# Router's logits from rows without the norm; scale and shift of the mixture's norm applied to gathered rows and to the residual

## The chip, the core and the metric

The kernel runs on one core of one Trainium2 chip. The time is that of one execution on the device in microseconds (us). The core has TensorE (PE, matrix products), VectorE (DVE), ScalarE (ACT), GpSimd (POOL) and SyncE (SP, whose queue starts the weight transfers), each with its own instruction stream, and 16 DMA engines. An instruction starts when those before it on its engine have gone and the semaphores that it waits for have come.

## The reference

Two layers work on 256 rows of width 2048. Each layer has a mixer and a mixture of experts, and after each of them the norm of the residual sum:

```
for i in range(2):
    mix = s5_mixer(h) if i == 0 else dsa_mixer(h)
    h = layer_norm(ALPHA * h + mix, ln_mix_g[i], ln_mix_b[i])
    ffn = hier_moe(h, ...)
    h = layer_norm(ALPHA * h + ffn, ln_ffn_g[i], ln_ffn_b[i])

def layer_norm(x, g, b): return (x - mean) * rsqrt(var + eps) * g + b

def hier_moe(x):
    group  = top 1 of softmax(x @ w_group + b_group)            # 4 groups
    expert = top 2 of softmax(x @ w_expert + b_expert) in group  # 8 each
    y = sum over the two experts: gate * (silu(x @ w_gate) * (x @ w_up)) @ w_down
```

All of it is in float32. There are 32 experts; each has three matrices of 2 MB.

## The kernel before

The rows stand in `acc`, 128 partitions by two halves `h` of 128 rows by 2048 columns. A plan list holds every weight tile of the program in the order of use, 2 MB each (4096 floats in each of 128 partitions). `issue()` starts the DMA of the next tile of the plan on SP's queue, into one of six ring slots (or a spare one in the mixture); SP waits there until the slot is released by the last reader of its old tile. `take()` hands the oldest tile to the code. In each layer the list holds, ahead of the mixture's 96 weight tiles, a tile `gb` with gain and bias of the mixer's norm, broadcast to all partitions (L143, L144).

The end of the mixer accumulates the output projection into `acc` and takes its statistics. Then the mixture begins (`moe`):

- *Norm.* `centre(q, h)` (L862) computes (acc - mean) * g on quarter q of the columns, `shift(q, h)` (L866) multiplies by `rs` = 1/sigma, from three Newton steps, and adds b: each eight times on 128x512 elements, on VectorE.
- *Logits.* While the quarters are being centred, TensorE transposes them (L222) into `xT` (ScalarE copies them from PSUM) and multiplies by the router weights `wr` of 36 columns (L1041) into `pl`. The factor `rs` and the bias are applied to the logits afterwards; `bw` (L1003, on GpSimd) is b times the router weights, whose column sums, by two products, go into `rbias`.
- *Split of the rows.* After each shift ScalarE rounds the rows to `xr` (L1058), and VectorE makes the rest `xl` (L1062). `keep_warm(p, n)` is n products without use.
- *Routing.* VectorE makes the logits `gl` and `el` (L1085, L1087), the group maximum `gr` (L1088), the choice (L1091 to L1104), positions within experts, and one-hot rows `ohr` (L1161).
- *Quads.* Eight quads of four experts: `gather` selects up to 32 rows for each expert by products of `xr`, `xl` with `ohr` and copies them to `xs` (L1178); `gate_up` (L1272) makes gate and up products, four experts side by side in columns of 32; `st_down` the down products; `scatter` adds them to `acc` (L1243). In quad 0 the scatter multiplies the old rows by ALPHA. `gate_up` runs over two halves of the contraction, in each over k = 0 (gate), 1 (up), and calls `issue()` twice after each k.

The order on each engine is that of the code, with lists of closures (`fill`, `during`) that put single steps between others.

Of the kernel before, what the change touches and what calls it, by code (L numbers as in the profile page):

```python
# [18 lines left out]
D = 2048  # L19
# [35 lines left out]
def kernel(ctx: ExitStack, tc: tile.TileContext, A, out):  # L55
# [85 lines left out]
    def gb(g, b, i):  # L141
        def f(t):
            nc.sync.dma_start(t[:, 0:D], dram(A[g], i * D, [[0, P], [1, D]]))  # L143
            nc.sync.dma_start(t[:, D:2 * D], dram(A[b], i * D, [[0, P], [1, D]]))  # L144
        return f

    def plan_s5():
# [12 lines left out]
        plan.append(gb("ln_mix_g", "ln_mix_b", 0))  # L160
# [682 lines left out]
    def ln_start(stt):  # L843
        if isinstance(stt, tuple):
            stt, gbt = stt
        else:
            gbt = take()
# [5 lines left out]
        return mv, ve, gbt[:, 0:D], gbt[:, D:2 * D]  # L853
# [91 lines left out]
    def plan_moe(li):  # L945
# [17 lines left out]
        i = RING - 1  # L963
# [6 lines left out]
    def moe(li, stt):  # L970

        with ExitStack() as ph:
# [14 lines left out]
            xT = [prp.tile([P, 4, L], F32, name="xT0")]  # L987
            wge = prp.tile([P, KC, 4], F32, name="wge")
            wex = prp.tile([P, KC, NEXP], F32, name="wex")
            wr = prp.tile([P, KC, 36], F32, name="wr")  # L990
            G.dma_start(wge, dram(A["moe_w_group"], li * D * 4, [[KC * 4, P], [4, KC], [1, 4]]))
            G.dma_start(wex, dram(A["moe_w_expert"], li * D * NEXP, [[KC * NEXP, P], [NEXP, KC], [1, NEXP]]))
            bT = prp.tile([P, KC], F32, name="bT")
            G.dma_start(bT, dram(A["ln_mix_b"], li * D, [[KC, P], [1, KC]]))
            rbias = prp.tile([P, 36], F32, name="rbias")
            G.dma_start(rbias[:, 0:32], dram(A["moe_b_expert"], li * 32, [[0, P], [1, 32]]))
            G.dma_start(rbias[:, 32:36], dram(A["moe_b_group"], li * 4, [[0, P], [1, 4]]))
# [4 lines left out]
            bw = prp.tile([P, KC, 36], F32, name="bw")  # L1002
            G.tensor_tensor(bw, wr, bT[:, :, None].to_broadcast([P, KC, 36]), op=OP.mult)  # L1003
# [17 lines left out]
            gl = sm("gl", [P, 2, 16]); el = sm("el", [P, 2, 40])  # L1021
            rp = sm("rp", [P, 2, 2, 8]); gr8 = sm("gr8", [P, 2, 8])
            for t in (gl, el, rp, gr8):
                G.memset(t, PAD)
            G.tensor_copy(id8, ident[0:8, 0:8])
# [3 lines left out]
            sbw = prp.tile([P, 36], F32, name="sbw")  # L1029
            xT += [prp.tile([P, 4, L], F32, name=f"xT{i}") for i in range(1, 4)]  # L1030
# [4 lines left out]
            junk, pbw = (pjk.tile([P, 512], F32, name="junk") for _ in range(2))  # L1035
            cut = lambda t, q: t.rearrange("p (k c) -> p k c", c=KC)[:, :, 4 * q:4 * q + 4]

            def logits(c0):
                for c in range(c0, c0 + 2):
                    for h in range(2):  # L1040
                        T.matmul(pl[:, h, 0:36], xT[c // 4][:, c % 4, h * 128:(h + 1) * 128], wr[:, c, :], start=c + h == 0,  # L1041
                                 stop=c == KC - 1, skip_group_check=True)


            for k in range(2):
                mm(pbw[:, 0:288], ones.to_broadcast([P, P]), bw[:, 8 * k:8 * k + 8].rearrange("p c n -> p (c n)"), k == 0, k == 1)
            keep_warm(pmm.tile([P, 512], F32, name="mm"), 8)
            centre, shift, rs = layer_norm(stt)
# [5 lines left out]
            def st_h(q):  # L1054
                for h in range(2):
                    shift(q, h)
                for h in range(2):
# [813 lines left out]
```

## Time and profile before

| | us |
|---|---|
| median of three runs | 1743.78 |
| lowest and highest | 1741.39, 1744.92 |
| the profiled execution's own time | 1746.2 |
| its span | 1744.6 |

Over the span TensorE is busy for 1500.0 us (86%), VectorE for 766.7 (44%), ScalarE for 498.3 (29%), GpSimd for 100.8 (6%); the mean granted clock of TensorE is 0.913. The DMA engines read 509.97 MB from HBM. TensorE's busy time includes products that run beside each other and ends that are modelled, so it is no measure of what is left to gain.

How to read the rows below: a timeline has the start in us from the span's start, the length, the engine, the line in the code, the operation, output<-inputs, elements, the count of instructions in the row, and in brackets the idle time ahead of it and who ended it. "x128" in one row are 128 records; a float32 product has two records. In the windows five pairs of busy time and count follow the length (PE, PEld, DVE, ACT, POOL); PEclk is the granted clock as a share of 2.4 GHz, behind it stand the DMA share and GB/s. Rows by form have busy us and the mean ns of one behind the first bar.

### The profile page before, as it was taken

To read this page: it belongs to the slowest core of one execution; us is meant where nothing else is said; L and a number is where in the kernel's file an instruction comes from. 1 tells how busy PE (TensorE), PEld (TensorE's weight loads), DVE (VectorE), ACT (ScalarE), POOL (GpSimd) and SP (SyncE) were. 2 spreads that over 40 slices of the span, in tenths; PEclk is the share of its full clock that TensorE was granted. 3 is DMA by queue.
4 is the path that set the end of the run, shared out by engine and by line. 5 is a ranking of instruction groups with operands and counts; after the bars stand their busy time and mean duration, and the time that the engine had idled before them with its cause. 6 is when DMAs were issued, how large, how long until landed. Compare 5 with 4: busy or idle time off the path is not lost. (4 is left out here: it accounts for less than half of the span.)

```text
span 1744.6 us, 28856 instructions
## 1 busy us (share of the span) xinstructions
PE 1500.0 (86%) x12151; PEld 1054.5 (60%) x12151; DVE 766.7 (44%) x1644; ACT 498.3 (29%) x1048; POOL 100.8 (6%) x225
## 2 busy tenths in 40 slices
PE   8899999999987777677788999999986887887687
PEld 7788888988643433343346998988743443433343
DVE  5788888666521112012116677976820220122015
ACT  2455554543310000000012464644410000010011
POOL 2111100001000000000001000500200000000000
PEclk8999999999887888898898999999988878888898
DMA  9545235655599999999996735344499999999994
GB/s 291 180 99 130 78 122 185 209 194 227 229 415 387 421 421 416 424 404 406 409 416 245 291 100 191 111 158 179 181 412 424 385 420 424 418 407 422 425 410 192
DMA packets 112939, 517.20 MB, mean 296 GB/s; under 512 B 8368, under 2 KB 41376, under 8 KB 71072
## 3 DMA queue, kind: packets, MB, share of 16 engines
q1 hardware_dynamic: 109664, 507.93, 73.5%
q0 software_dynamic: 3136, 7.31, 2.3%
q8 instruction: 100, 1.64, 0.4%
q14 instruction: 39, 0.32, 0.1%
HBM read 509.97 MB, written 5.24 MB: 295 GB/s over the span
## 5 line engine op out<-in xcount | busy, mean ns | idle before, releaser
L1272 PE MATMUL gu<-ring,xs 128*32 128x256 f32 x4096 | 319.5, 435 | 105.0 <-DMA ring<-in_moe_w_up_dram 84.9
L1272 PEld LDWEIGHTS gu<-ring,xs 128*32 128x32 f32 x4096 | 149.1, 124 | 263.3 <-DMA ring<-in_moe_w_up_dram 111.5
L64 PE MATMUL yd<-ring,hT 128*32 128x512 f32 x1024 | 190.8, 759 | 60.4 <-DMA ring<-in_moe_w_down_dram 59.4
L1197 DVE SCALAR_TENSOR_TENSOR hh<-gu,gsl,sg 128x256 f32<-128x256 f32 x16 | 7.7, 484 | 434.6 <-ACT sg L1195 434.6
L80 DVE TENSOR_TENSOR spl<-ring,spr 128x512 fp32r<-128x512 f32 x184 | 127.7, 696 | 83.7 <-ACT spr L79 80.3
L64 PE MATMUL mm<-ohr,xr 128*128 128x128 f32 x512 | 129.2, 294 | 32.5 <-DVE ohr L1161 19.1
L79 ACT ACTIVATE spr<-ring 128x512 fp32r<-128x512 f32 x184 | 115.7, 631 | 116.9 <-DVE spl L80 52.0
L64 PEld LDWEIGHTS yd<-ring,hT 128*32 128x32 f32 x1024 | 37.8, 131 | 180.1 <-DMA ring<-in_moe_w_down_dram 89.4
L80 DVE TENSOR_TENSOR yl<-yd,yr 128x512 fp32r<-128x512 f32 x64 | 44.3, 692 | 215.9 <-ACT yr L79 215.9
L64 PEld LDWEIGHTS mm<-ohr,xr 128*128 128x128 f32 x512 | 106.8, 209 | 45.1 <-issue 41.4
L64 PE MATMUL mm<-ohr,xl 128*128 128x128 f32 x512 | 128.5, 293 | 0.0
L1178 ACT ACTIVATE xs<-mm 128x512 f32<-128x512 f32 x64 | 38.2, 597 | 313.3 <-PE mm L64 313.3
L64 PE MATMUL u<-xT,ring 128*128 128x256 f32 x512 | 123.6, 396 | 2.1 <-DMA ring<-in_s_w_in_dram 1.6
L79 ACT ACTIVATE yr<-yd 128x512 fp32r<-128x512 f32 x64 | 38.3, 599 | 268.5 <-PE yd L64 268.5
L64 PEld LDWEIGHTS u<-xT,ring 128*128 128x128 f32 x512 | 98.7, 198 | 17.5 <-DMA ring<-in_s_w_in_dram 2.0
L64 PEld LDWEIGHTS mm<-ohr,xl 128*128 128x128 f32 x512 | 107.3, 209 | 0.1
L1195 ACT ACTIVATE sg<-gu 128x256 f32<-128x256 f32 x16 | 6.1, 384 | 254.1 <-PE gu L1272 254.1
L1243 DVE TENSOR_TENSOR acc<-acc,ps 128x512 f32<-128x512 f32 x112 | 72.7, 681 | 10.1 <-PE ps L64 10.0
L64 PE MATMUL ps<-yr,sc 128*128 128x512 f32 x128 | 59.2, 462 | 3.0 <-DVE acc L1243 2.0
L64 PEld LDWEIGHTS ps<-yr,sc 128*128 128x128 f32 x128 | 24.2, 189 | 61.2 <-issue 56.9
L1263 DVE TENSOR_SCALAR sc<-mm,slotp 128x256 fp32r<-128x256 f32 x16 | 7.7, 484 | 103.7 <-PE mm L64 103.7
L64 PE MATMUL mm<-spr,q 128*128 128x512 f32 x128 | 51.2, 400 | 0.0
(408 smaller groups left out, 2618.0 us busy)
## 6 DMA issues: line engine op xcount, KB each, us to landing
ring<-in_moe_w_gate_dram SPq DMA_DIRECT2D x128, 1024.0 KB, 16.0
ring<-in_moe_w_up_dram SPq DMA_DIRECT2D x128, 1024.0 KB, 19.6
ring<-in_moe_w_down_dram SPq DMA_DIRECT2D x56, 2048.0 KB, 24.6
ring<-in_s_w_glu_dram SPq DMA_DIRECT2D x8, 2048.0 KB, 9.4
ring<-in_s_w_out_dram SPq DMA_DIRECT2D x8, 2048.0 KB, 8.3
ring<-in_moe_w_down_dram SPq DMA_DIRECT2D x16, 1024.0 KB, 19.9
ring<-in_dsa_w_out_dram SPq DMA_DIRECT2D x8, 2048.0 KB, 8.0
ring<-in_s_w_in_dram SPq DMA_DIRECT2D x7, 2048.0 KB, 10.6
```

The lines of the kernel that those rows point to most:

```text
L64: T.matmul(o, l, r, start=start, stop=stop)
L79: S.activation(dst[0], src, AF.Copy)
L80: V.tensor_tensor(dst[1], src, dst[0].bitcast(F32), op=OP.subtract)
L1178: S.activation(xs[:, 4 * q:4 * q + 4], p.rearrange("p (a b) -> p a b", a=4), AF.Copy)
L1195: S.activation(sg, gu[:, 0:FF], AF.Silu)
L1197: V.scalar_tensor_tensor(hh, gu[:, FF:2 * FF], g, sg, op0=OP.mult, op1=OP.mult)
L1243: V.tensor_tensor(acc[:, h, bs], acc[:, h, bs], ps, op=OP.add)
L1263: V.tensor_scalar(scs[qd], p[:, 0:L], slotp, None, op0=OP.is_equal)
L1272: T.matmul(gu[es, k * FF:(k + 1) * FF], xss[qd][:, 8 * half + c, es], w[e // 2][:, e % 2, c, :], start=half + c + k == 0, stop=half == 1 a ...
```

## The change

The logits are taken from the rows as they are: with wr = g * w, x the raw row, m its mean, the logit is rs * (x @ wr - m * sum(wr)) + sum(b * w) + bias. The rows themselves get only (x - m) * rs; gain and bias come later.

- *Router weights.* GpSimd makes `wr` = w * g and `wb` = w * b, laid out in 44 columns padded to 64, and adds up 16 parts of each to one (`sw`); a product with ones gives the column sums in all partitions. ScalarE's two copies into `wr` go.
- *Logits.* Transposes of `acc` start after the statistics; four products of a block go alternately to partitions 0 and 64 of `plT`, with the weights as the fixed operand (64 columns) and 256 rows moving. `plS` is its copy, and two products with `sel` (the identity on both halves) bring it back to rows, `pl`. 12 `keep_warm` products follow where there were 16, and the 8 ahead of the transposes go.
- *Norm.* Four operations of 128x1024 on VectorE (`st_z`) replace 16 of 128x512.
- *Gathered rows.* Each copy of 128x512 becomes four of 128x128 with gain and bias per partition (`gTc`); in the first two gathers two of the four are on VectorE.
- *Residual.* In quad 0, during k = 0 of the second half, `residual(c - 8)` runs after each of the eight steps: four products spread ALPHA * g or ALPHA * b over the partitions, two VectorE operations apply it to `acc`. GpSimd prepares the two vectors (`mix_parts`). The scatter of quad 0 becomes the plain sum.
- *Tiles.* The `gb` tile leaves the plan, and so does the `issue()` behind the shifts; the spare tile is the seventh of the mixture instead of the sixth.

```diff
@@ plans
-        plan.append(gb("ln_mix_g", "ln_mix_b", 0))
...
-        i = RING - 1
+        i = RING
@@ moe
-            S.activation(wr[:, :, 0:32], wex, AF.Copy)
-            S.activation(wr[:, :, 32:36], wge, AF.Copy)
+            gTc = sm("gTc", [P, 2, KC])
+            for i, n in enumerate(("ln_mix_g", "ln_mix_b")):
+                G.dma_start(gTc[:, i], dram(A[n], li * D, [[KC, P], [1, KC]]))
+            wr = prp.tile([P, KC, 64], F32, name="wr")
+            wb = prp.tile([P, KC, 44], F32, name="wb")
+            G.memset(wr, 0.0)
+            G.memset(wb, 0.0)
+            for i, t in ((0, wr), (1, wb)):
+                for w, a, n in ((wex, 0, 32), (wge, 40, 4)):
+                    G.tensor_tensor(t[:, :, a:a + n], w, gbT[:, i, :, None].to_broadcast([P, KC, n]), op=OP.mult)
...
-            G.tensor_tensor(bw, wr, bT[:, :, None].to_broadcast([P, KC, 36]), op=OP.mult)
+            G.tensor_tensor(sel, ident[:, 0:56], ident[:, 64:120], op=OP.add)
+            sw = prp.tile([P, 8, 2, 44], F32, name="sw")
+            for i, t in ((0, wr), (1, wb)):
+                G.tensor_tensor(sw[:, :, i], t[:, 0:8, 0:44], t[:, 8:16, 0:44], op=OP.add)
+            for n in (4, 2, 1):
+                G.tensor_tensor(sw[:, 0:n], sw[:, 0:n], sw[:, n:2 * n], op=OP.add)
...
+            gs56 = prp.tile([P, 56], F32, name="gs56")
+            G.memset(gs56, 0.0)
...
+            def logits(b):
+                for c in range(4 * b, 4 * b + 4):
+                    o = 64 * (c % 2)
+                    T.matmul(plT[o:o + 64, 0:L], wr[:, c, :], xT[b][:, c % 4, :], start=c < 2, stop=c >= KC - 2,
+                             skip_group_check=True)
...
+            def sums():
+                V.tensor_copy(gs56[:, 0:44], junk[:, 0:44])
+                V.tensor_tensor(rbias[:, 0:44], rbias[:, 0:44], junk[:, 44:88], op=OP.add)
...
-            keep_warm(junk, 16)
-            for q in range(4):
-                st_h(q)
-            issue()
+            keep_warm(plT, 12)
...
+            def st_z(h):
+                for k in range(2):
+                    s = slice(k * 1024, (k + 1) * 1024)
+                    V.tensor_scalar(acc[:, h, s], acc[:, h, s], mv[:, h, 0:1], rs[:, h:h + 1], op0=OP.subtract, op1=OP.mult)
...
+            st_z(0)
+            st_z(1)
+            sums()
...
+                V.scalar_tensor_tensor(lg[:, h], gs56, nm[:, h:h + 1], pl[:, h, 0:56], op0=OP.mult, op1=OP.add)
...
+                V.scalar_tensor_tensor(lg[:, h], lg[:, h], rs[:, h:h + 1], rbias, op0=OP.mult, op1=OP.add)
@@ gather
-                S.activation(xs[:, 4 * q:4 * q + 4], p.rearrange("p (a b) -> p a b", a=4), AF.Copy)
+                for c in range(4):
+                    k = 4 * q + c
+                    g, b = gTc[:, 0, k:k + 1], gTc[:, 1, k:k + 1]
+                    if first and c % 2:
+                        V.tensor_scalar(xs[:, k], p[:, c * P:(c + 1) * P], g, b, op0=OP.mult, op1=OP.add)
+                    else:
+                        S.activation(xs[:, k], p[:, c * P:(c + 1) * P], AF.Identity, scale=g, bias=b)
@@ quad 0
+            def residual(k):
+                b, i = divmod(k, 2)
+                p = pmm.tile([P, 512], F32, name="mm")
+                for j in range(2):
+                    for x in range(2):
+                        mm(p[:, j * 256:(j + 1) * 256], id8[:, 2 * b + j:2 * b + j + 1].to_broadcast([8, P]),
+                           mixp[x][:, i * 256:(i + 1) * 256], x == 0, x == 1)
+                for h in range(2):
+                    a = acc[:, h, b * CB:(b + 1) * CB]
+                    V.tensor_tensor(a, a, p, op=OP.add if i else OP.mult)
...
-                    gate_up(0, 1)
+                    gate_up(0, 1, lambda c: residual(c - 8))
```

The instructions of GpSimd at the beginning of layer 0's mixture, before. `gb_4484` holds gain and bias of the later norm (L1007), `slot_4507` a counting row.

```order
L996 DMA rbias<-in_moe_b_expert_dram 128x32
L997 DMA rbias<-in_moe_b_group_dram 128x4
L1001 MEMSET ones 128x1
L1003 TENSOR_TENSOR bw<-wr,bT 128x576
L1007 DMA gb_4484<-in_ln_ffn_g_dram 8x256
L1007 DMA gb_4484<-in_ln_ffn_b_dram 8x256
L1009 IOTA slot_4507 128x64
```

After the change the same place has these rows, from the DMA of `gTc` on:

```order
L995 DMA gTc<-in_ln_mix_g_dram 128x16
L995 DMA gTc<-in_ln_mix_b_dram 128x16
L1000 MEMSET wr 128x1024
L1001 MEMSET wb 128x704
L1004 TENSOR_TENSOR wr<-wex,gbT 128x16x32
L1004 TENSOR_TENSOR wr<-wge,gbT 128x16x4
L1004 TENSOR_TENSOR wb<-wex,gbT 128x16x32
L1004 TENSOR_TENSOR wb<-wge,gbT 128x16x4
L1006 MEMSET ones 128x1
L1008 TENSOR_TENSOR sel<-ident 128x56
L1011 TENSOR_TENSOR sw<-wr 128x8x44
```

The single product `bw` has become two DMAs and nine more instructions up to `sw`. Three further sums into `sw`, the two DMAs of the later norm, the small constants and then `MEMSET gs_4541 128x56` follow; before, nothing of the logits stood behind `bw`.

TensorE, from the last product of layer 0's output projection on, before:

```order
L64 MATMUL mm<-spl,sTr 128x512
L64 MATMUL junk<-bw,ones 128x288 x2
L64 MATMUL mm<-ident 128x128 x8
L222 MATMUL mm<-ident,acc 128x128 x8
L1041 MATMUL pl<-wr,xT_4485 128x36 x4
L222 MATMUL mm<-ident,acc 128x128 x4
L1041 MATMUL pl<-wr,xT_4485 128x36 x4
L222 MATMUL mm<-ident,acc 128x128 x4
L1041 MATMUL pl<-wr,xT_4533 128x36 x4
L222 MATMUL mm<-ident,acc 128x128 x4
```

And after; `junk<-xT, wr` are the logits' products into `plT`, a tile on one PSUM buffer of that name:

```order
L64 MATMUL mm<-spl,sTr 128x512
L1064 MATMUL mm<-ident,acc 128x128 x16
L1053 MATMUL junk<-xT_4546,wr 64x256 x4
L1064 MATMUL mm<-ident,acc 128x128 x8
L1053 MATMUL junk<-xT_4547,wr 64x256 x4
L1064 MATMUL mm<-ident,acc 128x128 x8
L1053 MATMUL junk<-xT_4548,wr 64x256 x4
L64 MATMUL junk<-sw,ones 128x88
L1053 MATMUL junk<-xT_4549,wr 64x256 x4
L64 MATMUL pl<-sel,plS 128x56 x2
L64 MATMUL junk<-ident 128x128 x12
```

The 16 first transposes follow the projection at once, ahead of any logits; sixteen logits products stand where there were 32, then the two small products with `sel`.

VectorE, from the last Newton step to the group maximum, before:

```order
L840 SCALAR_TENSOR_TENSOR rs_y<-rs_t,rs_y 128x2
L862 SCALAR_TENSOR_TENSOR acc<-acc,ln_mv,ring 128x128x4 x4
L1073 TENSOR_REDUCE sbw<-junk 128x36
L1074 TENSOR_TENSOR rbias<-rbias,sbw 128x36
L866 SCALAR_TENSOR_TENSOR acc<-acc,rs_y,ring 128x128x4 x8
L1085 SCALAR_TENSOR_TENSOR gl<-pl,rs_y,rbias 128x4 x2
L1087 SCALAR_TENSOR_TENSOR el<-pl,rs_y,rbias 128x32 x2
L1088 TENSOR_REDUCE gr_4524<-gl 128x2
```

And after:

```order
L833 SCALAR_TENSOR_TENSOR rs_y<-rs_t,rs_y 128x2
L1090 TENSOR_SCALAR acc<-acc,ln_mv,rs_y 128x1024 x4
L1073 COPY gs_4541<-junk 128x44
L1074 TENSOR_TENSOR rbias<-rbias,junk 128x44
L1106 SCALAR_TENSOR_TENSOR lg<-gs_4541,nm,pl 128x56 x2
L1108 SCALAR_TENSOR_TENSOR lg<-lg,rs_y,rbias 128x56 x2
L1109 TENSOR_REDUCE gr_4538<-lg 128x2
```

The centre and shift rows are gone, among them the four between the Newton steps; four operations on 1024 columns, which wait for the transposes, stand ahead of the sums and the logits.

## Rows read from the trace of the kernel before

**Rows 1.** Windows of layer 0: stretch, length, busy by engine, PEclk, DMA share, GB/s

```profile
438.00:446.00 8.00, 8.00 (x72) 8.00 (x72) 7.93 (x20) 5.19 (x7) 0.00 (x0) 1.00 0.01 4
...
452.00:463.00 11.00, 11.00 (x122) 7.13 (x124) 7.99 (x26) 4.73 (x10) 0.00 (x0) 0.69 0.09 14
463.00:501.00 38.00, 32.31 (x318) 17.99 (x310) 7.46 (x20) 4.85 (x9) 0.00 (x0) 0.87 1.00 422
...
505.00:900.00 395.00, 300.96 (x2720) 155.74 (x2724) 59.13 (x122) 36.35 (x66) 0.00 (x0) 0.86 0.99 412
```

**Rows 2.** Timeline of SP in layer 0

```profile
445.19 17.05 SPq L926 DMA_DIRECT2D ring<-in_moe_w_up_dram  x4
...
461.43 0.80 SPq L926 DMA_DIRECT2D ring<-in_moe_w_up_dram  x2
462.33 3.36 SPq L942 DMA_DIRECT2D ring<-in_moe_w_down_dram  x3
...
475.17 0.33 SPq L942 DMA_DIRECT2D ring<-in_moe_w_down_dram  x1
```

**Rows 3.** Timeline of VectorE (DVE), router of layer 0

```profile
436.53 2.73 DVE L862 SCALAR_TENSOR_TENSOR acc<-acc,ln_mv,ring 128x512 f32<-128x512 f32 x4
...
439.78 5.38 DVE L866 SCALAR_TENSOR_TENSOR acc<-acc,rs_y,ring 128x512 f32<-128x512 f32 x8
...
445.66 0.15 DVE L1088 TENSOR_REDUCE gr<-gl 128x2 f32<-128x8 f32 x1
```

**Rows 4.** Timeline of TensorE (PE), router and first gather of layer 0

```profile
428.44 0.39 PE L64 MATMUL mm<-spl,sTr 128*128 128x512 f32 x1
...
450.59 0.30 PE L64 MATMUL mm<-ohr,xr 128*128 128x128 f32 x1 [1.73 <-DVE ohr L1161]
...
452.63 0.27 PE L64 MATMUL mm<-ohr,xr 128*128 128x128 f32 x1
...
469.79 8.80 PE L1272 MATMUL gu<-ring,xs 128*32 128x256 f32 x128
```

**Rows 5.** Timeline of GpSimd (POOL), layer 0

```profile
428.91 0.19 POOL L1009 IOTA slot<- 128x64 f32 x1 [0.79 <-PE mm L64]
...
430.93 0.18 POOL L1025 CAST id<-ident 8x8 fp32r<-8x8 f32 x1
```

**Rows 6.** Groups of instructions by form, whole span: busy us, mean ns

```profile
L1272 PE MATMUL gu<-ring,xs 128*32 128x256 f32 x4096 | 319.5, 435 | 105.0 <-DMA ring<-in_moe_w_up_dram 84.9 <-DMA ring<-in_moe_w_gate_dram 20.1
...
L64 PE MATMUL u<-xT,ring 128*128 128x256 f32 x512 | 123.6, 396 | 2.1 <-DMA ring<-in_s_w_in_dram 1.6 <-ACT uT L388 0.5
...
L1730 POOL TENSOR_TENSOR hk<-hk,idx 128x256 f32<-128x256 f32 x16 | 12.3, 772 | 1.3
...
L1003 POOL TENSOR_TENSOR bw<-wr,bT 128x576 f32<-128x576 f32 x2 | 2.3, 1157 | 79.4 <-ACT wr L999 79.4
...
L481 POOL MEMSET eb<- 128x512 f32 x3 | 1.4, 514 | 0.0
...
L1646 DVE TENSOR_SCALAR cc<-cc,rs_y 128x512 f32<-128x512 f32 x2 | 0.9, 480 | 0.0
...
L347 ACT ACTIVATE kk<-iot,cmag,pp 128x128 f32<-128x128 f32 x64 | 30.9, 483 | 0.2 <-DVE p L577 0.2
```

**Rows 7.** Timelines of GpSimd, TensorE, VectorE and SP, router of layer 1

```profile
1226.00 0.54 POOL L991 DMA_DIRECT2D wge<-in_moe_w_group_dram  x1 [88.93 <-PE mm L64]
...
1239.12 1.59 POOL L1027 TENSOR_TENSOR gbl<-gb,gbr 8x512 fp32r<-8x512 f32 x1
...
1231.12 0.40 PE L64 MATMUL mm<-spl,q 128*128 128x512 f32 x1
...
1237.83 4.10 DVE L862 SCALAR_TENSOR_TENSOR acc<-acc,ln_mv,ring 128x512 f32<-128x512 f32 x4
...
1248.32 0.15 DVE L1088 TENSOR_REDUCE gr<-gl 128x2 f32<-128x8 f32 x1
...
1263.91 0.80 SPq L926 DMA_DIRECT2D ring<-in_moe_w_up_dram  x2
```

More of the change, by code (lines that the diff above doesn't have):

```diff
@@ L843, in ln_start, with ln_moments @@
     def ln_start(stt):
[L844 to L847, printed above, removed]
+        stt, gbt = stt
+        mv, ve = ln_moments(stt)
+        return mv, ve, gbt[:, 0:D], gbt[:, D:2 * D]
+    def ln_moments(stt):
         mv = lnp.tile([P, 2, 2], F32, name="ln_mv")
@@ L1027, in moe @@
             G.tensor_tensor(gbl, gb8, gbr.bitcast(F32), op=OP.subtract)
-            sbw = prp.tile([P, 36], F32, name="sbw")
-            xT += [prp.tile([P, 4, L], F32, name=f"xT{i}") for i in range(1, 4)]
+            xT = [prp.tile([P, 4, L], F32, name=f"xT{i}", tag="xT", bufs=2) for i in range(4)]
             xr = one.tile([P, 2, D], F32R, name="xr")
@@ L1034, in moe @@
             pjk = pool(pre, "mjk", 2, side="right", **PS)
[L1035 to L1042, printed above, removed]
@@ L1045, in moe @@
[L1045 to L1048, printed above, removed]
+            junk, plT = (pjk.tile([P, 512], F32, name="junk") for _ in range(2))
+            def logits(b):
[3 more added lines that the diff above has]
+                             skip_group_check=True)
@@ new lines, in moe @@
+            mv, ve = ln_moments(stt)
+            for b in range(NBLK):
+                for c in range(0, 4, 2):
+                    p = pmm.tile([P, 512], F32, name="mm")
+                    for c2 in range(2):
+                        for h in range(2):
+                            T.transpose(p[:, c2 * 256 + h * 128:c2 * 256 + (h + 1) * 128],
+                                        acc[:, h, b * CB + c + c2:(b + 1) * CB:4], ident)
+                    S.activation(xT[b][:, c:c + 2, :], p.rearrange("p (a b) -> p a b", a=2), AF.Copy)
+                if b:
+                    logits(b - 1)
@@ new lines, in moe @@
+            mm(junk[:, 0:88], ones.to_broadcast([P, P]), sw[:, 0].rearrange("p i n -> p (i n)"), True, True)
+            nm = sm("nm", [P, 2])
+            def sums():
+                V.tensor_copy(gs56[:, 0:44], junk[:, 0:44])
+                V.tensor_tensor(rbias[:, 0:44], rbias[:, 0:44], junk[:, 44:88], op=OP.add)
+            rs = newton_rsqrt(ve, 2, [lambda: V.tensor_scalar(nm, mv[:, :, 0], -1.0, None, op0=OP.mult)])
+            logits(NBLK - 1)
+            plS = prp.tile([P, L], F32, name="plS")
@@ L1051, in moe @@
+            S.activation(plS, plT[:, 0:L], AF.Copy)
+            for h in range(2):
+                mm(pl[:, h, 0:56], plS[:, h * 128:(h + 1) * 128], sel, True, True)
+            keep_warm(plT, 12)
             xcut = lambda t, h, q: t[:, h].rearrange("p (c k) -> p c k", c=KC)[:, 4 * q:4 * q + 4]
             ccut = lambda t, h, q: t[:, h].rearrange("p (k c) -> p c k", c=KC)[:, 4 * q:4 * q + 4]
[L1054 to L1057, printed above, removed]
-                    S.activation(xcut(xr, h, q), ccut(acc, h, q), AF.Copy)
+            def st_z(h):
+                for k in range(2):
+                    s = slice(k * 1024, (k + 1) * 1024)
+                    V.tensor_scalar(acc[:, h, s], acc[:, h, s], mv[:, h, 0:1], rs[:, h:h + 1], op0=OP.subtract, op1=OP.mult)
@@ L1166, in xs_tile, with gather @@
                 return wk.tile([P, KC, P], F32, name="xs")
-            def gather(ohr, q, xs):
+            def gather(ohr, q, xs, first=False):
                 p = pmm.tile([P, 512], F32, name="mm")
@@ L1284, in settle @@
                     for h in halves:
[L1285 removed]
+                        scatter(y, scs[qd], b, h)
                     if halves[-1]:
@@ L1370, in moe @@
             for q in range(2):
-                gather(ohs[0], q, xss[0])
+                gather(ohs[0], q, xss[0], True)
+            mixp = mix_parts()
             gate_up(0, 0)
```

67 lines of the change are left out of this document (29 added, 38 removed).

## The prediction

> **What bounds the kernel now.** I read the busy share of the DMA queues over the span first, then windows around the router of the first mixture, then the timelines of SP, VectorE, TensorE and GpSimd there, and last the prices by form. The mixture is a stream of weights: from 463 to 501 us the DMA engines are busy all the time (share 1.00, 422 GB/s), and from 505 to 900 they still are (0.99, 412 GB/s), while TensorE is busy for 301 of those 395 us [rows 1]. The router before it lets the stream dry up: from 438 to 446 the share is 0.01 and from 452 to 463 it is 0.09 [rows 1]. All ring slots are then full of weights that nobody has used. The first slot comes free when the first quarter of quad 0's gate and up products is done: SP issues the next weights at 461.43 us in layer 0 and at 1263.91 in layer 1 [rows 2, 7]. Behind that point the time of a layer is that of its bytes, so whatever moves these two issues moves the end by the same amount. The refill of the norm's slot at 445.19 [rows 2] only fills one more slot in a hole; after the change a seventh weight tile is loaded ahead instead, so at the first release seven tiles are there in both kernels and the same bytes are still to come.
>
> What leads to that issue? In layer 0 TensorE ends the output projection at 428.83 (428.44 + 0.39) [rows 4]. VectorE then works almost without a pause: statistics, centre (the last four in 2.73 us), shift (eight in 5.38 us), and only then the group maximum `gr` at 445.66 [rows 3]. From `gr` the routing chain reaches the one-hot rows and the gather starts at 450.59, waiting for VectorE [rows 4]. From `gr` to the issue there are 461.43 - 445.66 = 15.8 us, in layer 1 1263.91 - 1248.32 = 15.6 us [rows 2, 3, 7]. I take this stretch over, up to the clock (below), and ask how early `gr` can stand.
>
> **What goes, and what is late next.** Sixteen centre and shift operations of about 0.7 us leave VectorE, four subtract-multiply operations of 128x1024 come. A price for these: 0.48 us for 128x512 [rows 6]; doubled, 0.96 us, so 3.8 us for four against some 11 us. But the logits no longer wait for the centred rows, and the four operations wait for the transposes, which read the same rows.
>
> TensorE's new order is transposes of blocks 0 and 1, logits of block 0, and so on. The logits wait for `wr`, which GpSimd now makes by itself. In layer 0 GpSimd's next step in the program waits for the last product of the projection, as the first one after the DMAs does today at 428.91, idle "<-PE mm" [rows 5]; in the new order that step is the DMA of `gTc`, so everything for the router's weights stands behind 428.9. The sum by rows: two DMAs at 0.54 [rows 7] 1.1; setting `wr` and `wb` to zero, 1728 columns, by 514 ns for 512 [rows 6] about 1.7; then `wr` = 576 columns, the size of the old `bw` at 1.16 [rows 6], with two instructions 1.35. `wr` stands at 428.9 + 4.1 = 433.0. Next `wb` 1.35, `ones` and `sel` 0.4, the sums `sw` of 352, 352, 352, 176 and 88 columns by the same 2 ns a column 0.8 + 0.8 + 0.8 + 0.5 + 0.3 = 3.2 and 0.3 of gaps: 438.3. Then two DMAs 1.1, the small constants about 2.0 (the old ones ran from 428.91 to 431.1 [rows 5], and two memsets of them are gone), and `gs56` at last: 441.5. VectorE's copy into `gs56` waits for that memset.
>
> TensorE in layer 0: logits of block 0 at 433.0. A product with 32 columns takes 319.5 / 4096 = 0.08 us beside three others, and a full-width product of 256 columns 123.6 / 512 = 0.24 us [rows 6]. The new ones (64 columns, two beside each other) have no row; the ends are half of 0.24 and 0.24 for each record, two records a product: 1.0 or 1.9 us for a block's four. I take 1.0, the side-by-side end, since the row nearest in form (the `gu` one, at different partitions) shows its neighbours running together. Then transposes of blocks 2 and 3 at 1.0 each: the last transposes end near 437, the last logits near 439, and with a copy of 0.4 and two small products `pl` is there near 440.5. The four new operations run from 437 to 440.9. So GpSimd's 441.5 is last, by 0.6: copy, sum and four small operations of 0.2 take 1.2, `gr` at 442.7 instead of 445.66: 2.9 us gained.
>
> Layer 1: GpSimd starts its DMAs at 1226.0, before the projection's end at 1231.52 [rows 7], and `gTc` does not wait for that end. Eight DMAs at 0.54 and a memset 4.5, then the same work: `wr` at 1233.5, `sw` at 1238.8, `gs56` at 1241.9; the last logits follow the transposes, `pl` near 1241; the four operations from 1238 to 1241.9. `gr` at 1243.1 instead of 1248.32: 5.2 us.
>
> Together 8.1. Two things take from it. *GpSimd's price*: `hk` on two full operands took 772 ns for 256 columns, 3 ns a column [rows 6], and beside VectorE it can be more. At 3 ns the products and sums are 50 per cent dearer: 1.3 us in each layer. I take half, 0.7 each, since `bw` (multiply with a broadcast) is nearer in kind than `hk`; ends 0 and 1.3. *The clock*: TensorE loses full speed in the gather. In layer 0 its products start 0.11 us apart from 450.59 to 452.63, after a pause of 1.73 us (18 steps, [rows 4]); the stretch 452 to 463 has a granted clock of 0.69 [rows 1], a mean between the level of 1.2 GHz (0.5) and that of 2.4. After the change the keep-warm products are 12 instead of 16, and TensorE has waits for `wr` and `pl` that it lacked. If those first products ran at the lower level too, at 0.22 a step, some 20 of them would be 0.11 slower: 2.2 us; if the clock is as before, 0. I take 1.0 a layer. Sum: -8.1 + 1.4 + 2.0 = -4.7 us. The profiled execution took 1746.2, 1.6 over its span of 1744.6; it would be 1741.5. The median shown, 1743.78, lies 2.4 lower, and I put the same gain on it: 1739.1.
>
> **What I cost at nothing.** The residual's gain and bias in quad 0: eight steps with two VectorE operations on 128x512, at 0.67 as a shift of that size (5.38 / 8 [rows 3]), and four products. VectorE is busy for 7.5 of 38 us there [rows 1]. A step costs 1.35 us, more than the 0.55 of a step of the gate and up products (sixteen in 8.8 [rows 4]), and with two buffers the last of the eight waits for six of VectorE's steps: 8.1 us instead of eight times 0.55, so the release at 475.17 [rows 2] comes some 4 us later. Four tiles were issued from 461.43 to 465.69 [rows 2] and one lasts about 5.0 us (2.1 MB at 422 GB/s), so the queue is not empty before 481 to 483: covered by about 2 us. Without cover it is that delay, 4 us in each layer. The gather's copies in four pieces with scale and bias: four at 0.48 [rows 6] on ScalarE, which is busy for 4.85 of 38 us [rows 1]; in the first two gathers half go to VectorE, so that its first piece is there before a whole copy would be. The two broadcasts of gain and bias, 2 MB in each layer, went through the queue while it was filling the ring: nothing.
>
> **Rivals.**
> *GpSimd is stretched beside VectorE* (the slower side). In layer 1 the four centre operations that ran beside GpSimd's `gbl` (1.59) took 4.10 us [rows 7]; the same four in layer 0, without it, 2.73 [rows 3]. So a factor of 1.5 is seen when both work. If GpSimd's compute, 10 us in the chain up to `gs56`, costs that factor, since VectorE's statistics, Newton steps and four operations run beside it, `gs56` comes 5 us later: 2.9 - 5.0 = 2.1 lost in layer 0, 5.2 - 5.0 = 0.2 gained in layer 1, and with the clock's 2.0 the kernel is 4 us slower: 1748. It decides from a factor of about 1.3, where 2 x 3 us eat what the clock leaves of 8.1. Against: most of VectorE's operations in that stretch are on two columns.
> By the Trainium skill, "SBUF — State Buffer", section "SBUF: two separate sides", GpSimd and a VectorE operation with two SBUF inputs (or in a two-port mode) lock one pair of ports for a whole instruction, and the loser blocks. The 4.10 beside 2.73 agrees; the rule would make this rival's price the length of each overlapping VectorE operation.
> *The logits' pairs do not run together.* Then each block costs 1.9 instead of 1.0, `pl` comes near 444 and 1243.3, `gr` at 444.2 and 1245.3: 1.5 + 3.0 gained, 2.0 lost with the clock: -2.5, 1741.3. For: no row shows 64-column pairs.
> *Quad 0 is throttled by the residual.* If a step costs twice as much, 2.7 us (the products wait for VectorE with two buffers, and both for each other), six steps are 16.2 us, the release at 475.17 comes 12 later instead of 4, and behind 2 us of cover the queue is empty for 6 us in each layer: 1739 + 12 = 1751. Against: one VectorE operation has nothing else beside it there.
> *GpSimd is not last and the clock is kept.* The shifts are then bounded by the four operations: 3.5 and 5.5, or 9 in all: 1734.8.
> *The change does not shorten anything*: `gr` would have to stay behind the same length of VectorE work, which the order excludes; no chance of its own.
>
> **How the numbers follow.** Forecast 0.50 (its own range 1736.5 to 1742); pairs serial 0.15; GpSimd stretched 0.13; quad 0 throttled 0.09; nothing lost 0.13. A difference of 0.2 per cent, 3.5 us, is about what a measurement of this kernel tells from no change, so faster means below 1740.3. Of the forecast 0.38 lies there, of the serial case 0.03, and all of the last, 0.13: 0.54. Slower than 1747.3: 0.09 of the throttled case and 0.06 of the stretched: 0.15. The rest, 0.31, is within. The range from 1733 to 1748 holds all but the throttled case and the outer parts of the first and last.
>
> **What would show it.** In the changed profile SP's issue at 461.43 stands near 458 to 460 and the one at 1263.91 near 1259 to 1261, with a DMA share of 0.98 or more behind them. VectorE's copy into `gs56` waits for GpSimd, and `sw` ends near 438. The first logits wait for GpSimd's `wr`. A logits block of four takes 1.0 us. The residual's steps come 1.35 us apart with no hole in the DMA share near 480. I am wrong if the issue comes early and the end does not, which would mean that the stream is broken later, or if `gr` stands near 442 and the issue near 461, which would put the loss on the clock in the gather.

## The result and the profile after

The changed kernel takes 1762.76 us (median of five, 1755.45 to 1767.58) against 1742.72 for the kernel before in the same sessions: ratio 1.0116, 95% interval 1.0088 to 1.0143, some 20 us slower. I had forecast 1739.1, 4.7 faster, in a range from 1733 to 1748. The profiled execution took 1759.32 with a span of 1757.7, 13.1 over that of before: the traces show 13 of the 20 us.

Up to the end of layer 0's projection the two traces differ by 1 us: it ends at 427.79 after (427.39 + 0.40) and at 428.83 before. From there on, times behind this end are compared. TensorE's timeline shows the router and the first gather of layer 0 in the changed kernel, and one of the residual's steps from its gate products to the next ones:

```profile
427.39 0.40 PE L64 MATMUL mm<-spl,sTr 128*128 128x512 f32 x1
...
432.17 1.08 PE L1053 MATMUL junk<-xT,wr 128*64 128x256 f32 x8 [1.99 <-POOL wr L1004]
...
446.42 0.20 PE L64 MATMUL mm<-ab,oneb 128*1 128x32 bf16 x2 [3.12 <-DVE am L1125]
...
449.65 0.45 PE L64 MATMUL mm<-ohr,xr 128*128 128x128 f32 x1 [2.48 <-DVE ohr L1182]
449.89 0.41 PE L64 MATMUL mm<-ohr,xl 128*128 128x128 f32 x1
...
456.64 8.15 PE L1319 MATMUL gu<-ring,xs 128*32 128x256 f32 x128
...
474.88 1.08 PE L1319 MATMUL gu<-ring,xs 128*32 128x256 f32 x8
475.89 0.58 PE L64 MATMUL mm<-yr,id 8*128 8x256 f32 x1
...
477.04 1.08 PE L1319 MATMUL gu<-ring,xs 128*32 128x256 f32 x8
```

The gate products of the kernel before begin here:

```profile
455.62 9.22 PE L1272 MATMUL gu<-ring,xs 128*32 128x256 f32 x128
```

The gather starts 21.86 us behind the projection's end, where it was 21.76 (450.59 - 428.83, [rows 4]): nothing gained. Its products start 0.21 to 0.24 apart from the first on, and the gate products start at 28.85 (456.64 - 427.79) instead of 26.79. SP's timeline of layer 0 and of layer 1, the counterpart of [rows 2, 7]:

```profile
461.38 0.81 SPq L920 DMA_DIRECT2D ring<-in_moe_w_up_dram  x2
...
484.62 0.33 SPq L936 DMA_DIRECT2D ring<-in_moe_w_down_dram  x1
...
1266.13 1.32 SPq L920 DMA_DIRECT2D ring<-in_moe_w_up_dram  x2
```

The first issue comes 33.6 us behind the projection's end in layer 0 (32.6 before) and 33.0 in layer 1 (32.4; the projection ends at 1233.17 after). The next one that waits for a release, at 475.17 before, stands at 484.62. What that does to the stream is in the windows of layer 0, with the columns of [rows 1]:

```profile
449.00:457.00 8.00, 7.35 (x36) 7.10 (x40) 5.12 (x10) 1.17 (x3) 1.74 (x2) 0.50 0.01 3
463.00:472.00 9.00, 8.13 (x97) 5.88 (x89) 3.63 (x19) 4.72 (x13) 0.00 (x0) 1.00 1.00 417
472.00:482.00 10.00, 10.00 (x64) 5.19 (x60) 6.47 (x11) 0.00 (x0) 0.00 (x0) 0.52 1.00 424
482.00:488.00 6.00, 6.00 (x46) 3.23 (x44) 3.32 (x6) 0.00 (x0) 0.00 (x0) 0.50 0.54 178
...
506.00:511.00 5.00, 5.00 (x36) 1.89 (x28) 2.80 (x6) 1.20 (x2) 0.00 (x0) 1.00 0.05 18
```

Where before the DMA share was 1.00 from 463 to 501 and 0.99 from 505 on, two holes, stretches in which the DMA engines have little to do, stand: 482 to 488 (0.54) and 506 to 511 (0.05). Layer 1 has the same two (1286 to 1292 with 0.39, 1312 to 1317 with 0.13). TensorE is at the lower clock level in the residual's stretch (0.52 and 0.50) and is busy all the time, while VectorE waits 0.87 us for it in each step (row 474.98 below): TensorE, and not VectorE, sets the pace.

VectorE and GpSimd in layer 0's router after (the counterparts of [rows 3, 5]), first VectorE:

```profile
430.99 0.89 DVE L827 TENSOR_TENSOR rs_t<-rs_y 128x2 f32<-128x2 f32 x1
...
441.76 0.20 DVE L1073 COPY gs<-junk 128x44 f32<-128x44 f32 x1 [1.86 <-POOL gs L1037]
...
442.08 0.46 DVE L1106 SCALAR_TENSOR_TENSOR lg<-gs,nm,pl 128x56 f32<-128x56 f32 x2
442.45 1.47 DVE L1108 SCALAR_TENSOR_TENSOR lg<-lg,rs_y,rbias 128x56 f32<-128x56 f32 x2
443.96 0.16 DVE L1109 TENSOR_REDUCE gr<-lg 128x2 f32<-128x8 f32 x1
...
448.77 0.93 DVE L1182 TENSOR_TENSOR ohr<-slot,pos 128x128 fp32r<-128x128 f32 x2
...
474.98 1.29 DVE L1256 TENSOR_TENSOR acc<-acc,mm 128x512 f32<-128x512 f32 x2 [0.87 <-PE mm L64]
```

and GpSimd:

```profile
428.08 0.54 POOL L995 DMA_DIRECT2D gTc<-in_ln_mix_g_dram  x1 [82.99 <-PE mm L64]
...
437.85 0.70 POOL L1017 DMA_DIRECT2D gb<-in_ln_ffn_g_dram  x1
...
441.59 0.14 POOL L1037 MEMSET gs<- 128x56 f32 x1
...
442.49 1.36 POOL L1040 TENSOR_TENSOR gbl<-gb,gbr 8x512 fp32r<-8x512 f32 x1
```

`gr` waits for `gs` (the tile of `gs56`), as forecast, but 1.3 us later than forecast (it is ready 13.94 us behind the projection's end, not 12.67), and the sums and logits behind it take 2.2 us where I had 1.2. So `gr` comes 16.17 us behind the end instead of 16.83.

### The profile page after: what moved, and what is told of

It reads as the page before. It is cut to its first block, busy times and chain, and to the rows that moved or that the text cites. A ratio compares the mean times of both kernels' runs of the same rounds, so it can differ in the third digit from the quotient of the medians.

```text
span 1757.7 us, 29020 instructions
## 1 busy us (share of the span) xinstructions
PE 1508.2 (86%) x12107; PEld 1053.4 (60%) x12107; DVE 784.4 (45%) x1662; ACT 552.6 (31%) x1230; POOL 131.1 (7%) x263
## 5 line engine op out<-in xcount | busy, mean ns | idle before, releaser
L1319 PE MATMUL gu<-ring,xs 128*32 128x256 f32 x4096 | 325.1, 440 | 108.7 <-DMA ring<-in_moe_w_up_dram 82.7
L64 PE MATMUL yd<-ring,hT 128*32 128x512 f32 x1024 | 186.1, 751 | 42.5 <-DMA ring<-in_moe_w_down_dram 41.6
L1205 ACT ACTIVATE xs<-mm,gTc 128x128 f32<-128x128 f32 x248 | 94.1, 458 | 277.7 <-PE mm L64 275.8
L1290 DVE TENSOR_TENSOR acc<-acc,ps 128x512 f32<-128x512 f32 x128 | 83.0, 681 | 11.7 <-PE ps L64 11.7
```

The source lines that it names most:

```text
L64: T.matmul(o, l, r, start=start, stop=stop)
L1205: S.activation(xs[:, k], p[:, c * P:(c + 1) * P], AF.Identity, scale=g, bias=b)
L1290: V.tensor_tensor(acc[:, h, bs], acc[:, h, bs], ps, op=OP.add)
L1319: T.matmul(gu[es, k * FF:(k + 1) * FF], xss[qd][:, 8 * half + c, es], w[e // 2][:, e % 2, c, :], start=half + c + k == 0, stop=half == 1 a ...
```

## Experiments

The theory (A): the residual's steps in quad 0, paced by TensorE at the lower clock level, hold back the releases and break the stream twice; a smaller part is that the router is not earlier. The rival (B): the four-piece copies of the gathered rows, or the late first issue alone, break it. Each kernel ran beside the kernel before on the same chip; a time is compared with that of before by its ratio, with the 95% interval in brackets. The distances to the changed kernel, whose runs are not those of the experiments, are differences of medians. "The release" is SP's issue at 484.62, which waits for a slot.

**The residual left out.**

```diff
-                    gate_up(0, 1, lambda c: residual(c - 8))
+                    gate_up(0, 1)
```

> The residual's eight steps in quad 0 are left out (gain and bias are not applied to the residual, so its values differ); all the rest is the changed kernel. Theory A (the steps, at 2.16 us each with TensorE at the lower clock level, hold back quad 0's slots and break the weight stream twice): the release that stands at 484.6 in the changed kernel comes back to 474 to 476, both holes in the DMA share (482 to 488 and 506 to 511) are gone, 9 us of stream in each layer come back, of which layer 0 may give some back at its end: 1762.8 - 10 to 18 = 1745 to 1753. Theory B (the four-piece copies of the gathered rows, or the later first issue, break the stream): the hole at 506 to 511 stays and the time stays above 1756.

Measured: 1748.64, ratio 1.0034 (1.0018 to 1.0051), 14 us under the changed kernel. Its SP timeline and windows of layer 0:

```profile
474.84 0.33 SPq L936 DMA_DIRECT2D ring<-in_moe_w_down_dram  x1
```

```profile
480.00:488.00 8.00, 5.66 (x47) 4.45 (x46) 1.10 (x5) 3.29 (x9) 0.00 (x0) 0.95 0.99 420
500.00:512.00 12.00, 10.79 (x142) 5.11 (x138) 4.14 (x7) 0.60 (x1) 0.00 (x0) 1.00 0.98 395
560.00:570.00 10.00, 10.00 (x69) 3.05 (x61) 4.46 (x7) 1.79 (x3) 0.00 (x0) 0.89 0.27 114
```

Both holes are gone with the residual and nothing else, so neither the four-piece copies nor a late first issue, which is later still here, make them. It is still 6 us slower than before: the first issue is 2.4 us (layer 0) and 0.5 us (layer 1) later, and a hole that the kernel before has in quad 1 too (560 to 570, share 0.63) is deeper here, 0.27; what deepens it stays open.

**Operands of 128 rows for the residual.**

```diff
-                        mm(..., id8[:, 2 * b + j:2 * b + j + 1].to_broadcast([8, P]), mixp[x][...], ...)
+                        mm(..., id128[:, 2 * b + j:2 * b + j + 1].to_broadcast([P, P]), mixp[x][...], ...)
```

> The residual's products get operands of 128 rows instead of 8 (the rows beyond 8 are zero), same columns and same count. Theory A1 (TensorE falls to the lower level in this stretch because of these thin products): the granted clock stays at or near 1.0 through 472 to 486, a step takes about 1.35 us (VectorE's two sums) instead of 2.16, the late release comes near 478 to 479 instead of 484.6, the time 6 to 12 us under the changed kernel: 1751 to 1757. Theory A2 (the clock falls because of the waits and the short bursts, whatever the rows): the clock is 0.5 as before, steps 2.16 us, time as the changed kernel, 1762 +- 4.

The tiles are set to zero first; count and columns of the products stay. Measured: 1749.92, ratio 1.0037 (1.0016 to 1.0059), 13 us under the changed kernel for rows of zeros. Windows of layer 0, and VectorE's sums there:

```profile
470.00:477.00 7.00, 6.55 (x37) 3.67 (x38) 3.47 (x9) 1.18 (x4) 0.00 (x0) 0.53 1.01 431
477.00:487.00 10.00, 10.00 (x124) 5.92 (x128) 7.56 (x13) 0.00 (x0) 0.00 (x0) 0.99 0.95 374
```

```profile
475.82 1.28 DVE L1261 TENSOR_TENSOR acc<-acc,mm 128x512 f32<-128x512 f32 x2 [0.88 <-PE mm L64]
477.75 7.45 DVE L1261 TENSOR_TENSOR acc<-acc,mm 128x512 f32<-128x512 f32 x12 [0.64 <-PE mm L64]
```

The clock falls here too, ahead of the first of these products, but it comes back in the middle of the steps (in layer 1 earlier), and from then on VectorE does six of them in 7.45 us, 1.24 a step without a pause; before that a step takes 2.16 as in the changed kernel. The price that I had put on a step (1.35) holds at full clock only. So the clock lies between the two that I expected, and the time even under the lower one's 1751 to 1757: the release comes at 483.24, 54.1 us behind the projection's end (56.8 in the changed kernel), and in layer 1 at 52.4 (57.7). The first hole is nearly gone, the second is left (504 to 510, share 0.30).

**Two products a step.** Main part and remainder of gain and bias in one operand of 128 rows:

```diff
-                        mm(..., id8[...], mixp[x][...], x == 0, x == 1)      # for x in range(2)
+                    mm(..., id128[...], mixp[:, i * 256:(i + 1) * 256], True, True)
```

> Main part and remainder of gain and bias stand in one operand (rows 0 to 7 and 32 to 39 of 128), so a residual step has two products instead of four. Theory A: TensorE's share of a step falls from 1.15 to 0.6 us at the lower level, and a step is 1.7 us at that level or 1.3 (VectorE) at the full one; the late release comes 4 to 7 us earlier than 484.6, the time is 6 to 14 us under the changed kernel: 1749 to 1757. Theory B (residual not at fault): no change, 1762 +- 4.

Measured: 1745.49, ratio 1.0019 (1.0002 to 1.0037), 17 us under the changed kernel, better than expected. The release stands 50.9 us behind the projection's end (56.8), as expected, and the clock of 470 to 480 is 0.90. A hole remains at 502 to 506 (share 0.35).

**Router weights first.** On GpSimd, the zeroing of `gs56` ahead of the DMA of `gTc`, and both behind `sw`:

```diff
-            gTc = sm("gTc", [P, 2, KC])   # and its two DMAs, ahead of wr
...
                 G.tensor_tensor(sw[:, 0:n], sw[:, 0:n], sw[:, n:2 * n], op=OP.add)
+            gs56 = prp.tile([P, 56], F32, name="gs56")
+            G.memset(gs56, 0.0)
+            gTc = sm("gTc", [P, 2, KC])   # and its two DMAs
```

> GpSimd makes wr, wb, sw and clears gs56 before the DMA of gTc, so that wr and wb no longer wait for the projection's end in layer 0, and in both layers gs56 is ready some 3 us earlier; the residual stays. If GpSimd's order sets gr (my step for the first issue): in layer 0 the wait of the first logits (1.99 us) goes, gr comes 2 to 4 us earlier than 443.96, the first issue 2 to 4 us before 461.38; in layer 1 1 to 2.5 us. By theory A the late release behind the residual then moves with it: time 3 to 6 us under the changed kernel, 1757 to 1760. If the clock in the gather or VectorE sets it instead: gr moves under 1 us and the time stays.

Measured: 1759.34, ratio 1.0102 (1.008 to 1.0125). GpSimd waits at `sel` instead, and in layer 0 three rows of GpSimd and VectorE read:

```profile
427.98 0.30 POOL L1005 TENSOR_TENSOR sel<-ident 128x56 f32<-128x56 f32 x1 [76.18 <-PE mm L64]
```

```profile
432.84 0.16 DVE L827 TENSOR_TENSOR rs_t<-rs_y 128x2 f32<-128x2 f32 x1
...
440.44 0.16 DVE L1109 TENSOR_REDUCE gr<-lg 128x2 f32<-128x8 f32 x1
```

`gr` is at 11.63 us behind the end, 4.5 earlier, and the first issue at 29.8 (33.6); in layer 1, where only `gs` is earlier, they gain 1.5 and 0.7. So GpSimd's order did set `gr`. The row at 432.84 is an operation on two columns while GpSimd issues DMAs: 0.16 us, where it took 0.89 in the changed kernel (430.99) beside GpSimd's products. That the time falls is not shown: the median is 3.4 us lower, by the ratios 2.4, and the two intervals overlap. The release behind the residual moves by 2.1 us only (54.8).

**Two products, spread over both k.**

```diff
-                    gate_up(0, 1, lambda c: residual(c - 8))
+                    gate_up(0, 1, lambda c: residual((c - 8) // 2) if c % 2 else None, 16)
```

> As the run with two products a step, but the eight steps are spread over the sixteen steps of both k of quad 0's second half, one behind every second. Theory A: VectorE's 1.21 to 1.24 us a step are then covered by two steps of gate and up products (1.1 us and 0.3 for the residual), so the releases come as without a residual but 1 to 2 us (50.9 us behind the projection's end in layer 0 becomes 47 to 49), and the short hole in the DMA share some 74 to 77 us behind the projection's end goes. Time 2 to 5 us under the kernel with two products: 1740 to 1744, about the kernel before. If the rest of the loss lies elsewhere (four-piece copies, the later first issue alone): no change against 1745.5.

Measured: 1747.66, ratio 1.0022 (1.0009 to 1.0035): the release comes at 48.1 as expected, but the hole at 502 to 506 stays (share 0.38), and the interval is that of the run with two products. My expectation failed for the hole and the time: the hole ends with the next release, behind quad 0's first down products, which stands 76.1 us behind the projection's end here and 76.2 with two products beside one k.

**A filled TensorE ahead of the first gather**, in the changed kernel:

```diff
-            keep_warm(plT, 12)
+            keep_warm(plT, 24)
...
             mm(pt[0:32, 384:512], ab[:, 1], identb, True, True)
+            keep_warm(junk, 16)
```

> The changed kernel with 24 keep-warm products ahead of the ranks (12 before) and 16 behind them, nothing else. If the granted clock in the first gather is set by TensorE's idle time ahead of it: the gather's products start 0.11 us apart for at least the first 20 of 64 (0.213 from the first in the changed kernel), the gate and up products start 1.5 to 4 us earlier than 28.85 us behind the projection's end (layer 0), the first issue 1 to 3 us earlier. If the waits on VectorE alone set the gather's end: no change above 0.5 us. The holes behind the residual stay, time 1755 to 1764.

Measured: one run, 1753.86. TensorE and windows of layer 0:

```profile
450.21 0.31 PE L64 MATMUL mm<-ohr,xr 128*128 128x128 f32 x1
450.35 0.28 PE L64 MATMUL mm<-ohr,xl 128*128 128x128 f32 x1
...
453.91 2.37 PE L1320 MATMUL gu<-ring,xs 128*32 128x256 f32 x40
```

```profile
450.00:454.00 4.00, 4.00 (x41) 3.93 (x43) 3.30 (x6) 0.92 (x2) 0.05 (x1) 1.00 0.01 2
458.00:467.00 9.00, 8.13 (x104) 6.01 (x97) 5.35 (x26) 5.27 (x15) 0.00 (x0) 1.00 0.94 377
467.00:482.00 15.00, 15.00 (x87) 8.04 (x88) 8.99 (x14) 0.00 (x0) 0.00 (x0) 0.53 0.79 334
```

The gather takes 3.7 us instead of 7.0, and the first issue comes at 30.3 and 28.7 us behind the end (33.6 and 33.0), more than expected. The clock then falls 0.9 us behind the residual's first product (467.00), although TensorE was at 2.4 GHz and busy for 8.13 of 9 us ahead of it. The time is under the 1755 to 1764 expected, but one run tells little of it.

**The residual beside the second k.**

```diff
-                        if during and k == 0:
+                        if during and k == at:      # at = 1
```

> The residual's eight steps, with four products each as in the changed kernel, go beside the second k (up) of quad 0's second half instead of the first. Theory A with two places: the release of the first k comes back to 46 to 48 us behind the projection's end, so the hole at 482 to 488 goes; quad 0's down products start as late as in the changed kernel (498.8), so the hole at 506 to 511 stays: 4 to 7 us in each layer come back, 1750 to 1758. If the second hole is only the echo of the first, both go: 1744 to 1750. If the residual's delay at the first release did not matter: 1762 +- 4.

Measured: 1753.48, ratio 1.0076 (1.0047 to 1.0104), as expected of two places. A window of layer 0:

```profile
498.00:504.00 6.00, 6.00 (x45) 2.23 (x48) 3.79 (x7) 1.20 (x2) 0.00 (x0) 1.00 0.19 68
```

The release is at 45.4 and the first hole gone; from 498 to 504 the share is 0.19. So the second hole is no echo of the first: one comes from the slots of the first k, the other behind the late down products. In layer 0 of this run the clock stayed at 1.00 through the residual (470 to 479), in layer 1 it fell: the one case of ten stretches with products of 8 rows that kept full clock.

**All four repairs**: two products, spread, router weights first, filled TensorE.

> Two products a step, spread over both k, router weights first on GpSimd, and 24 keep-warm products ahead of the ranks and 16 behind them, where the changed kernel has 12 and none. If my account is whole, the first issue comes 27 to 30 us behind the projection's end in layer 0 (33.6 in the changed kernel, 32.6 before) and 29 to 31.5 in layer 1 (33.0, 32.4), and no hole follows: 1734 to 1740, 3 to 9 us under the kernel before. If only the residual mattered, it stands where the kernel with spread products stands, 1740 to 1744.

Measured: 1736.31, ratio 0.9956 (0.994 to 0.9972): faster than both kernels. First issue at 27.3 and 28.8, as expected; smaller holes are left, against the expectation (494 to 498 with a share of 0.80, 1290 to 1300 with 0.69). The gather now waited for the keep-warm products.

**Keep-warm trimmed** to 17 and 7:

> The kernel with all four repairs, its keep-warm products cut from 24 and 16 to 17 and 7: in that kernel the gather waited 2.8 us for them (they end at 448.65, the one-hot rows are ready at 445.85). If that wait is the only thing between: the gather comes 2 to 3 us earlier in each layer, the clock in it stays at 1.0, the first issue at 24.5 to 26 us behind the projection's end in layer 0 (27.3) and 26 to 28 in layer 1 (28.8), time 3 to 6 us under 1736.3: 1730 to 1734. If the shorter filling loses the clock, the gather's products start 0.21 apart from early on and the gain is eaten: 1735 to 1739.

Measured: 1732.8, ratio 0.9933 (0.9912 to 0.9954), as expected. The gather moves from 19.9 to 16.7 us behind the end (layer 0). SP's first issue and the windows of layer 0:

```profile
453.09 1.09 SPq L920 DMA_DIRECT2D ring<-in_moe_w_up_dram  x2
```

```profile
445.00:453.00 8.00, 7.92 (x104) 6.17 (x106) 6.66 (x14) 4.14 (x7) 4.03 (x3) 1.00 0.02 5
455.00:493.00 38.00, 34.21 (x312) 20.38 (x303) 18.99 (x54) 10.73 (x28) 0.00 (x0) 0.87 1.01 424
493.00:497.00 4.00, 4.00 (x37) 1.50 (x36) 2.82 (x6) 0.60 (x1) 0.00 (x0) 1.00 0.59 186
```

The projection ends at 428.64 here, so the first issue is at 24.4, 8.2 us earlier than before the change; in layer 1 it is at 26.7. The gather of layer 0 runs at full clock, and of the holes 493 to 497 (0.59) is left, in layer 1 1284 to 1290 (0.54).

**One copy for each gather**, in the trimmed kernel:

```diff
-                for c in range(4):   # four pieces with gain and bias
+                S.activation(xs[:, 4 * q:4 * q + 4], p.rearrange("p (a b) -> p a b", a=4), AF.Copy)
```

> As the trimmed kernel, but each gather's copy is one operation of 128x512 without gain and bias (these are left out for the gathered rows, so the values differ). Theory A says that the four pieces (1.51 us on ScalarE instead of 0.60) are off the path: within 3 us of the trimmed kernel, holes as there. Rival B: the pieces hold back the gate products or quad 0's and 1's down products and so make the holes that remain at 70 to 80 us behind the projection's end; then these holes go and the time falls by 4 to 10 us.

Measured: 1730.4, ratio 0.9918 (0.989 to 0.9947), which overlaps the trimmed kernel's interval: the median is 2.4 us lower, and that is not clear of noise. The hole at 493 to 497 is still there, with a share of 0.72. So the pieces do not make it, and the 4 to 10 us of rival B do not come; a smaller price of the pieces is not excluded.

**Four thin products in the trimmed kernel.**

```diff
-                    mm(..., id128[...], mixp[:, i * 256:(i + 1) * 256], True, True)
+                        mm(..., id8[...], mixp[x][...], x == 0, x == 1)      # for x in range(2)
```

> As the trimmed kernel, but the residual has its four products of 8 rows a step again, spread over both k. If thin products take or keep TensorE at the lower level: the granted clock falls to 0.5 during the residual in both layers though it was 1.0 ahead of it, the sixteen steps take 16 us or more instead of 11, the second k's release comes 4 to 7 us later than in the trimmed kernel, time 4 to 10 us above it. If only the count of products matters and the clock holds: sixteen steps in 13.5 us at most, time 1 to 4 us above it.

Measured: 1758.14, ratio 1.0078 (1.0049 to 1.0107), 25 us above the trimmed kernel, far more than the 4 to 10 expected. Windows of layer 1, where the residual runs from 1270.15 to 1292:

```profile
1260.00:1270.00 10.00, 9.41 (x132) 6.89 (x124) 6.42 (x27) 5.26 (x15) 0.00 (x0) 1.00 0.87 336
1272.00:1292.00 20.00, 19.96 (x132) 10.04 (x124) 7.93 (x14) 0.38 (x1) 0.00 (x0) 0.50 1.00 421
1292.00:1302.00 10.00, 7.53 (x34) 7.26 (x35) 2.08 (x5) 2.38 (x7) 0.00 (x0) 0.50 0.98 399
1302.00:1316.00 14.00, 13.32 (x81) 4.80 (x81) 5.56 (x12) 2.80 (x7) 0.00 (x0) 0.77 0.05 19
```

A TensorE that is busy and at 2.4 GHz falls to 1.2 at 1270.9, 0.7 us behind the first thin product, and stays there beyond their end. The sixteen steps take 21.8 us, and behind them the stream stops for 14 us (share 0.05). Against the trimmed kernel count and rows of the products both differ here; only the run with operands of 128 rows changes the rows alone.

## Why the prediction was wrong

**The step that failed: "What I cost at nothing".** I priced a residual step by VectorE's two sums alone, 1.35 us, and set against it the gate products at full clock, 0.55. The four products of a step got no price, and the clock of this stretch was not asked for. Measured, VectorE's pair is 1.29 us and not the limit: TensorE works through 1.08 of gate products and 1.08 of thin products in each step of 2.16 at the lower level, so the release that I had 4 us late, with 2 us of queue to spare, comes 9.45 late on the clock of the profile, and the queue is empty from 482 on. The run without a residual gives 14 of the 20 us back, the one with full-height operands 13. The rest is in the main the router, whose first issue came later and not earlier: without the residual the kernel is still 6 us slower than before, where I had it 4.7 faster, and a part of that, the deeper hole of quad 1, stays open. The throttled quad 0 was a rival of mine, with 0.09 and 1751, and its empty queue did come; its mechanism (TensorE and VectorE waiting for each other) was not it, since TensorE waits for nobody there: busy for 10.00 of 10 us.

**A second hole that no sentence of mine had.** Quad 0's down products, before and after:

```profile
489.76 5.75 PE L64 MATMUL yd<-ring,hT 128*32 128x512 f32 x26 [3.45 <-DMA ring<-in_moe_w_down_dram]
```

```profile
498.79 5.34 PE L64 MATMUL yd<-ring,hT 128*32 128x512 f32 x32
```

They start at 498.8 where they had waited for their weights until 489.8, the first of their slots comes free at 510.1 instead of 501.5 (SP's next issue that waits), and the stream stops a second time. The run with the residual beside the second k separates the two.

**`gr` earlier by 2.9 and 5.2: mis-sized.** It came 0.66 and 1.85 us earlier relative to the projection's end. The mechanism was right, as the run with the router weights first shows (4.5 more in layer 0). GpSimd's chain was 1.3 us longer in layer 0 and 2.3 in layer 1, part of it DMA issues at 0.7 us instead of 0.54, and VectorE's own operations stretch beside it: the pair of logits operations took 1.47 us (442.45) where the pair ahead of it took 0.46, and it ends at 443.92, 0.07 behind GpSimd's `gbl` (442.49 to 443.85); `ohr` took 0.93 where it took 0.49 before. That is the rival "stretched beside VectorE" in kind, though on both engines; the Trainium skill, "SBUF — State Buffer", section "SBUF: two separate sides", says that the loser of their shared port pair blocks for the whole instruction, and the end of that pair agrees.

**The clock in the gather: 1.0 a layer, measured 2.0 and 1.8.** The bound of 2.2 was almost reached. All 32 products ran at 0.21, 7.0 us for the gather instead of 5.0. The run with a filled TensorE (3.7 us) shows that TensorE's idle time ahead of it did that: in layer 0 it waits 3.12 us for the ranks' input and 2.48 for the one-hot rows, before the change only 1.73 for the latter [rows 4].

**What was right.** Sixteen operations of VectorE did go, pairs of 64 columns do run beside each other (eight records in 1.08 us, 1.0 forecast), the first logits wait for `wr` and the copy into `gs56` for GpSimd, and behind the first issue the same weight tiles are still to come. The term that only the end would show, that a shift of the first issue is a shift of the end, fits the trimmed kernel: 8.2 and 5.7 us earlier, 12 us in time (8 to 15 by the interval), with a small hole in each layer.

**Open.** The profiled execution was 9.4 us behind that of before in the middle of layer 0's stream (an issue at 754.96 before, 764.33 after) and 1.65 behind at layer 1's projection; 2.3 of the difference is told below, where the rest came back is not shown. Why the clock falls ahead of the residual in some runs, with either height of the operands, is not shown either.

## What to carry to other kernels

Price a step that is woven into a matmul loop on both engines and at both clock levels, and ask what the new products do to the clock: with products on 8 of the 128 rows that a product sums over, whole stretches stood at half speed here, and zero rows up to full height brought the clock back within 5 us. A stream that lives on slot releases has as many places to break as there are releases; check each one against what is queued ahead of it, the down phase too. And when an engine off the path becomes the producer (GpSimd here), its instruction order is on the path, down to a memset that could stand anywhere.

## What was not expected of the hardware

Nine of ten stretches with products of 8 rows ran at 1.2 GHz. In five of the nine the clock was at 2.4 when the first such product came and fell 0.7 to 4.6 us behind it; in four it had fallen 0.6 to 2.1 us ahead of it. In all nine it stayed down to the last such product. With operands of 128 rows the clock fell ahead of the residual too in seven of twelve stretches, but came back 1.6 to 4.9 us behind its start in all seven; in five it held.

A VectorE operation on two columns can wait long beside GpSimd. At the start of the second mixer, VectorE in the kernel before and then GpSimd:

```profile
932.49 3.68 DVE L852 TENSOR_SCALAR ln_ve<-ln_mv 128x2 f32<-128x2 f32 x1
```

```profile
930.84 5.30 POOL L1481 TENSOR_TENSOR spl<-ring,spr 128x1168 fp32r<-128x1168 f32 x2
```

and the same operation of VectorE in the changed kernel, where GpSimd's pair runs from 932.17 to 937.54:

```profile
936.22 1.35 DVE L846 TENSOR_SCALAR ln_ve<-ln_mv 128x2 f32<-128x2 f32 x1
```

An addition on two columns lasted 3.68 us, and in both kernels it ends with GpSimd's pair (936.14 and 937.54). In the changed kernel it starts 3.7 us later than before and ends 1.4 later: that it came later against the pair gave 2.3 us back.
